# Sums of squares in an attention stage: transposes and a free-axis sum in place of products with a column of ones

## The chip, the core and the metric

The kernel runs on one core of a Trainium2 chip. The core has five engines, each with its own instruction queue that it works through in order: TensorE (PE in the profile; PEld is its loading of weights), VectorE (DVE), ScalarE (ACT), GpSimd (POOL) and SyncE (SP), which issues the DMAs. Engines wait for each other by semaphores. Products go into PSUM, eight banks of 128 x 512 float32. The metric is the time of one execution on the device in microseconds (us). The kernel before has a median of 1921.74 us over three runs (1920.86 to 1923.17).

## The reference

One layer: a normalised and modulated input of 1024 latent and 256 context tokens is projected, goes through two branches (A: a gated DeltaNet, B: differential attention), and both are merged. The change lies in branch B, behind the attention of each of the 8 heads:

```
def diff_attend(q, k, v, lam):              # per block of 128 queries
    s = jnp.einsum('bqhcd,bkhcd->bhcqk', qi, k) * scale     # c: two score maps
    p = jax.nn.softmax(s, axis=-1)
    attn = p[:, :, 0] - lam * p[:, :, 1]
    return jnp.einsum('bhqk,bkhv->bqhv', attn, v)           # 128 features a head
...
y_b = rms_norm(o_b, diff_norm_w) * (1.0 - lambda_init) * jax.nn.silu(z_b)
merged = g_a * (y_a @ w_oa) + g_b * (y_b @ w_ob)
```

`rms_norm(o_b)` needs, for each token and head, the sum of the squares of 128 features. How that sum is formed is what changes.

## The kernel before

The attention stage runs from about 1290 to 1750 us. A unit of work is a **tile**: 128 queries of one head, 64 tiles in all (8 heads of 8). Two tiles make a **pair**; there are 32 pairs, four to a head, counted here from the 1st to the 32nd. Head 0 has pairs 1 to 4, head 3 begins with pair 13, head 5 with pair 21, head 7 with pair 29.

A tile goes through these steps, and all of them are interleaved with other tiles:

- `scores` (L1615): 12 products `s` on TensorE, two for each of six pieces of 512, 512 and 256 keys for two score maps. VectorE moves each piece out of its bank with a scale and a minimum (`score_out`, L1642); three banks are shared.
- `soft` and `rel` (L1651, L1664): exponentials on ScalarE, small operations on VectorE.
- `scale` and `add` (L1673, L1681): one map scaled by -lambda times a ratio, on ScalarE or, for every fourth tile, on GpSimd, and the two added on GpSimd.
- `turns` (L1688): ten transposes `t` on TensorE, each of 128 x 128.
- `high` and `low` (L1706, L1718): ScalarE and VectorE split the transposed tile into two parts, `ah` and `al`.

A pair then goes through:

- `att_out` (L1726): 30 products `v` into the first 256 columns of a PSUM bank. This pool has one bank. Features lie on the partitions, the pair's 256 queries along the free axis.
- `out_pair` (L1743): ScalarE squares these 256 columns into `osq`.
- `gate_` (L1754): VectorE writes the gated output `oT`.
- `sum_` (L1763): the sum of squares over the partitions. TensorE multiplies each half of `osq` by a column of ones, `self.one`, into one column each of the same bank; VectorE scales the two columns, adds a small term `e2` and writes two columns of `ms`. With that and `oT` done, the bank is handed to the next pair (`self.vbank`).

After a head's fourth pair, `norm_` (L1786) raises `ms` to the power -0.5 on GpSimd (`bry`), transposes it on TensorE (`m<-ct,bry`), sends it through memory to every partition and multiplies `oT` by it.

Beside this runs `merge_` (L1870): 16 groups of 24 products `ma` of 512 columns, for branch A. They depend on little and fill TensorE between the steps of the attention. The last three groups are kept until all 64 tiles have been scored (`KEEP`, L1833, L1873). `merge_` and `norm_` take turns at one PSUM bank (`pbank`).

What sets the order is a planner in the kernel itself (`turn_flow`, L100). Each step is a generator that yields (engine, estimated time, dependencies, instruction); the planner keeps a clock for each engine and picks the step that can start earliest on it, with biases from `ABIAS`. So the numbers in a `yield` are no instructions, but a change of one of them, or one more step, may move all that follows. Two conditions hold steps back by plan alone: `over_` (L1760) lets the scores of head h begin only after the `norm_` of head h-2 has been planned to its end, and `norm_` needs the shared bank.

Of the kernel before, what the change touches and what calls it, by code (L numbers as in the profile page):

```python
# [12 lines left out]
ALU = mybir.AluOpType  # L13
AX = mybir.AxisListType
# [3 lines left out]
P = 128  # L18
# [11 lines left out]
W = 256  # L30
# [4 lines left out]
PE, DVE, ACT, POOL, DMA, ADMA, DV2, PL1 = range(8)  # L35
# [8 lines left out]
class Block:  # L44
# [1718 lines left out]
    def sum_(self, y, w, po, sq, t):  # L1763

        t0 = y["t"]
        e2 = self.a2.tile([P, 2], F32, tag="e2", name="e2")
        te = yield ACT, 0.13, [], lambda: self.nc.scalar.activation(e2, w["l0"][:, 0, t0:t0 + 2], AF.Square, scale=EPS ** 0.5)
        for j in range(2):
            t = yield PE, 0.11, [t], lambda: self.mm(po[:, W + j:W + j + 1], sq[:, j * P:(j + 1) * P], self.one)
        t = yield DVE, 0.075, [t, te], lambda: self.nc.vector.scalar_tensor_tensor(  # L1770
            w["ms"][:, t0:t0 + 2], po[:, W:W + 2], 1.0 / P, e2, ALU.mult, ALU.add)
        yield lambda: "o" in y
        self.vbank.append([t, y["o"]])
        if t0 == NL - 2:
            self.szfree = y["o"]
            self.norms.append((2 * y["i"] + 1, self.norm_(y["h"], w, t, y["o"])))
# [513 lines left out]
```

## Time and profile before

| | |
|---|---|
| median of three runs | 1921.74 us |
| the profiled execution, its span | 1923.5 us |
| TensorE busy | 1890.3 us (98%) |
| VectorE busy | 1458.9 us (76%) |
| ScalarE busy | 1079.6 us (56%) |
| GpSimd busy | 670.2 us (35%) |
| granted TensorE clock, mean | 0.998 |

The profile is of one execution. Its span, from the first to the last instruction, is 1.8 us above the median of the runs and within the three runs' spread by 0.4 us; there is no separate time around it in the profile. A row of the timeline has the start (us from the span's start), the duration, the engine, the line, the operation, the tiles as written<-read, the shape and how many instructions the row merges. A matmul's duration overlaps with the next one's, so what it occupies TensorE for is read from start to start. A row of the windows has, for each stretch, its length and the busy time of PE, PEld, DVE, ACT and POOL, then the granted clock, the DMA share and GB/s.

### The profile page before, as it was taken

To read this page: it belongs to the slowest core of one execution; us is meant where nothing else is said; L and a number is where in the kernel's file an instruction comes from. 1 tells how busy PE (TensorE), PEld (TensorE's weight loads), DVE (VectorE), ACT (ScalarE), POOL (GpSimd) and SP (SyncE) were. 2 spreads that over 40 slices of the span, in tenths; PEclk is the share of its full clock that TensorE was granted. 3 is DMA by queue.
4 is the path that set the end of the run, shared out by engine and by line. 5 is a ranking of instruction groups with operands and counts; after the bars stand their busy time and mean duration, and the time that the engine had idled before them with its cause. 6 is when DMAs were issued, how large, how long until landed. Compare 5 with 4: busy or idle time off the path is not lost.

```text
span 1923.5 us, 37549 instructions
## 1 busy us (share of the span) xinstructions
PE 1890.3 (98%) x13821; PEld 1663.8 (86%) x13821; DVE 1458.9 (76%) x3622; ACT 1079.6 (56%) x2241; POOL 670.2 (35%) x605
## 2 busy tenths in 40 slices
PE   7999999999999999999999999999999999999999
PEld 5988888899999998888888878888997988988887
DVE  5788998948886887767876756337996979995687
ACT  5553444426234563676776645548885868884222
POOL 2200000005541432343433232336666667672203
PEclk9999999999999999999999999999999999999999
DMA  9145534575546557667686555666436474226542
GB/s 337 62 134 113 140 92 123 132 205 170 175 132 204 156 194 229 231 196 251 198 274 203 196 179 157 205 227 232 136 122 212 159 241 159 84 89 217 181 161 88
DMA packets 383039, 336.39 MB, mean 175 GB/s; under 512 B 142609, under 2 KB 323443, under 8 KB 381831
## 3 DMA queue, kind: packets, MB, share of 16 engines
q1 hardware_dynamic: 382855, 333.99, 55.3%
q8 instruction: 109, 1.79, 0.4%
q14 instruction: 75, 0.61, 0.1%
HBM read 222.14 MB, written 111.79 MB: 174 GB/s over the span
## 4 chain that ended last, share of the span: by engine, by line
PE 56%; DVE 4%; ACT 2%; DMA 2%; issue 2%; POOL 1%; SPq 1%; ACTq 0%; DVEq 0%; POOLq 0%
PE mm L56 17%; PE s L56 7%; PE v L56 6%; PE chain L56 5%; PE mb L56 5%; PE ma L56 4%; PE x L56 3%; PE t L63 3%; PE out L56 3%; DVE S L1646 1%; PE gram L56 1%; PE z L56 1%; DVE al L1720 1%; DMA x<-xq 0%; ACT X L1310 0%
## 5 line engine op out<-in xcount | busy, mean ns | idle before, releaser
L56 PE MATMUL mm<-hs,wh 128*128 128x512 f32 (+1 forms) x2048 | 646.1, 389 | 1.2 <-ACT hs L453 1.2
L56 PEld LDWEIGHTS mm<-hs,wh 128*128 128x128 f32 x2048 | 371.9, 189 | 58.7 <-issue 2.0
L56 PE MATMUL mm<-hs,wl 128*128 128x512 f32 (+1 forms) x1024 | 397.8, 389 | 0.0
L56 PE MATMUL mm<-wh,hs 128*128 128x256 f32 (+1 forms) x1792 | 327.8, 283 | 0.8 <-ACT xc L649 0.6
L56 PEld LDWEIGHTS mm<-wh,hs 128*128 128x128 f32 x1792 | 276.8, 188 | 1.5 <-ACT xc L649 0.8
L56 PE MATMUL mm<-wl,hs 128*128 128x256 f32 (+1 forms) x896 | 253.6, 283 | 0.0
L1646 DVE TENSOR_SCALAR_CACHE_REDUCE S<-s,rsq 128x512 f32<-128x512 f32 (+1 forms) x384 | 239.0, 655 | 15.2 <-PE s L56 12.2
L1683 POOL TENSOR_TENSOR S<-S 128x1280 f32<-128x1280 f32 x64 | 188.9, 2957 | 92.0 <-ACT S L1676 90.8
L56 PEld LDWEIGHTS mm<-hs,wl 128*128 128x128 f32 x1024 | 193.9, 189 | 28.9 <-issue 0.9
L1659 ACT ACTIVATE S<-S,mn 128x1280 f32<-128x1280 f32 x128 | 175.2, 1371 | 51.1 <-DVE mn L1658 50.1
L56 PEld LDWEIGHTS mm<-wl,hs 128*128 128x128 f32 x896 | 168.8, 188 | 0.1
L661 DVE SCALAR_TENSOR_TENSOR ac<-xc,convT,ac 128x1284 f32<-128x1284 f32 (+1 forms) x96 | 138.8, 1448 | 14.1 <-ACT ac L659 13.5
L56 PE MATMUL s<-kk,qh 128*128 128x512 f32 (+1 forms) x384 | 142.1, 370 | 2.2 <-DVE S L1646 1.8
L56 PE MATMUL s<-kk,ql 128*128 128x512 f32 (+1 forms) x384 | 132.2, 356 | 0.0
L1720 DVE TENSOR_TENSOR al<-t,ah 128x512 fp32r<-128x512 f32 (+1 forms) x192 | 106.9, 595 | 7.0 <-ACT ah L1715 5.8
L646 POOL MEMSET xc<- 128x2 f32 (+1 forms) x64 | 3.5, 101 | 297.2 <-DMA gkk<-xc 117.7
L1231 DVE TENSOR_TENSOR tmp<-ab,ts 80x31 f32<-80x31 f32 (+15 forms) x248 | 94.1, 379 | 9.4 <-DMA ab<-da 3.8
L1364 POOL TENSOR_TENSOR x<-x,ct 128x256 f32<-128x256 f32 x64 | 47.7, 752 | 149.9 <-DMA x<-xq 107.9
L56 PE MATMUL ma<-y,wh 128*128 128x512 f32 x256 | 94.6, 414 | 1.8 <-DVE g L1893 1.8
L1233 DVE TENSOR_TENSOR ts<-ts,tmp 80x31 f32<-80x31 f32 (+15 forms) x248 | 91.3, 368 | 6.3
L1400 ACT ACTIVATE vd<-chain,edk 128x128 f32<-128x128 f32 x144 | 52.6, 371 | 76.5 <-PE chain L56 70.0
L1715 ACT CAST ah<-t 128x512 fp32r<-128x512 f32 (+1 forms) x192 | 88.1, 522 | 8.0 <-PE t L63 7.3
(307 smaller groups left out, 4356.2 us busy)
## 6 DMA issues: line engine op xcount, KB each, us to landing
wr<-in_w_in_dram SPq DMA_DIRECT2D x48, 512.0 KB, 5.8
hx<-in_w_in_dram SPq DMA_DIRECT2D x64, 256.0 KB, 4.7
x<-xq SPq DMA_DIRECT2D x64, 256.0 KB, 3.9
X<-gcd SPq DMA_DIRECT2D x8, 1280.0 KB, 10.6
kd<-col SPq DMA_DIRECT2D x40, 256.0 KB, 2.5
xq<-X SPq DMA_DIRECT2D x16, 640.0 KB, 4.5
kk<-kd SPq DMA_DIRECT2D x16, 640.0 KB, 5.7
kq<-gkq SPq DMA_DIRECT2D x8, 1152.0 KB, 8.4
```

Of the source, the lines that this page charges most:

```text
L56: self.nc.tensor.matmul(out, lhsT, rhs, start=start, stop=stop)
L63: self.nc.tensor.transpose(out, src, self.ident[:src.shape[0], :src.shape[0]])
L661: t = yield DV2, 1.21e-3 * wd, [t], lambda: nc.vector.scalar_tensor_tensor(ac[:, :wd], xc[:, j:j + wd], self.convw(j, x["ct"]), ac[:, :wd] ...
L1231: t = yield DV2, n * w / 960.0 + 0.08, [t if j else self.later(t, 2.5), t1], lambda: V.tensor_tensor(tv, ab[:, j + 1:, j:j + 1].to_broadca ...
L1233: t = yield DV2, n * w / 960.0 + 0.08, [t, t1], lambda: V.tensor_tensor(ts[:, j + 1:, :w], ts[:, j + 1:, :w], tv, ALU.subtract)
L1364: u["tqk"] = yield POOL, 0.72, [u["tx"]], lambda: nc.gpsimd.tensor_tensor(x[:, 1], x[:, 1], (self.up, self.lo)[d].unsqueeze(1).to_broadcas ...
L1400: td = yield ACT, 0.251, [t], lambda: nc.scalar.activation(vd, pc[:, 1], AF.Copy, scale=self.edk[:, c, g:g + 1])
L1646: e = yield DVE, 0.675 if m == 512 else 0.408, [e, self.sfree[c].get(n - 4 + c)], lambda: self.nc.vector.tensor_scalar(x["S"][c][:, o:o + ...
L1659: x["x"].append((yield ACT, 1.36, [e], lambda: nc.scalar.activation(S, S, AF.Exp, bias=x["mn"][:, c:c + 1], scale=-1.0, accum_out=w["l0"][ ...
L1683: e = yield POOL, 2.9, [e], lambda: self.nc.gpsimd.tensor_tensor(S0, S0, S1, ALU.add)
L1715: e = yield ACT, 0.48 if nb == 4 else 0.27, [t, y["old", k]], lambda: self.nc.scalar.copy(y["ah", k][:, :, q], pv)
L1720: t = yield DVE, 0.603 if k < 2 else 0.322, [e, y["old", k]], lambda: self.nc.vector.tensor_tensor(y["al", k][:, :, q], pv, y["ah", k][:, ...
```

## The change

In `sum_` the two products with a column of ones become two transposes of 128 x 128 (through `tr`, L62). They write 256 columns of the same bank, with the queries on the partitions; a new VectorE reduction sums them along the free axis into `ms`, and the scaling with the small term becomes an operation on `ms` alone. The bank is handed on after the reduction (`tb`) and `oT`.

```
         for j in range(2):
-            t = yield PE, 0.11, [t], lambda: self.mm(po[:, W + j:W + j + 1], sq[:, j * P:(j + 1) * P], self.one)
-        t = yield DVE, 0.075, [t, te], lambda: self.nc.vector.scalar_tensor_tensor(
-            w["ms"][:, t0:t0 + 2], po[:, W:W + 2], 1.0 / P, e2, ALU.mult, ALU.add)
+            t = yield PE, 0.109, [t], lambda: self.tr(po[:, W + j * P:W + j * P + P], sq[:, j * P:(j + 1) * P])
+        ms = w["ms"][:, t0:t0 + 2]
+        tb = t = yield DVE, 0.35, [t], lambda: self.nc.vector.tensor_reduce(
+            ms, po[:, W:2 * W].rearrange("p (j c) -> p j c", j=2), AX.X, ALU.add)
+        t = yield DVE, 0.075, [t, te], lambda: self.nc.vector.scalar_tensor_tensor(ms, ms, 1.0 / P, e2, ALU.mult, ALU.add)
         yield lambda: "o" in y
-        self.vbank.append([t, y["o"]])
+        self.vbank.append([tb, y["o"]])
```

The planner makes another order of the whole stage from this. Three places show it; in the rows, `s`, `t`, `v`, `ma` are the products and transposes named above, and x10 is ten in a row.

VectorE behind the 4th pair, before:

```order
L1646 TENSOR_SCALAR S,m_16021<-s,rsq 128x256
L1757 SCALAR_TENSOR_TENSOR oT<-v,dg,sz 128x256
L1720 TENSOR_TENSOR al<-t,ah 128x4x128 x2
L1770 SCALAR_TENSOR_TENSOR ms<-v,e_16107 128x2
L1720 TENSOR_TENSOR al<-t,ah 128x2x128
```

The same place in the changed kernel:

```order
L1646 TENSOR_SCALAR S,m_16026<-s,rsq 128x256
L1757 SCALAR_TENSOR_TENSOR oT<-v,dg,sz 128x256
L1720 TENSOR_TENSOR al<-t,ah 128x4x128 x2
L1771 TENSOR_REDUCE ms<-v 128x2
L1720 TENSOR_TENSOR al<-t,ah 128x2x128
L1773 SCALAR_TENSOR_TENSOR ms<-ms,e_16111 128x2
```

The reduction stands where the scaling stood, and the scaling comes one operation later.

TensorE between the 18th and the 19th pair's products, near the end of head 4, before:

```order
L56 MATMUL v<-ct,osq 128x1 x2
L56 MATMUL ma<-y,wl 128x512
L56 MATMUL ma<-y,wh 128x512 x2
L56 MATMUL ma<-y,wl 128x512
L56 MATMUL ma<-y,wh 128x512
L63 MATMUL t<-ct,S 128x128 x4
L56 MATMUL ma<-y,wh 128x512
L63 MATMUL t<-ct,S 128x128 x6
L56 MATMUL ma<-y,wl 128x512
L56 MATMUL ma<-y,wh 128x512 x2
L56 MATMUL ma<-y,wl 128x512
L56 MATMUL ma<-y,wh 128x512 x2
```

The same place in the changed kernel, up to the 19th pair's first product:

```order
L63 MATMUL v<-ct,osq 128x128 x2
L63 MATMUL t<-ct,S 128x128 x4
L63 MATMUL m<-ct,bry 8x128
L63 MATMUL t<-ct,S 128x128 x6
L56 MATMUL v<-ah,vh 128x256
```

Twelve products `ma` stood among the transposes; now none does, and the transpose of `norm_` has moved in.

TensorE behind the 27th pair, in head 6, before:

```order
L56 MATMUL v<-ct,osq 128x1 x2
L56 MATMUL ma<-y,wl 128x512
L63 MATMUL t<-ct,S 128x128 x4
L56 MATMUL ma<-y,wh 128x512
L63 MATMUL t<-ct,S 128x128 x6
L56 MATMUL ma<-y,wh 128x512
L56 MATMUL s<-kk,qh 128x512
L56 MATMUL s<-kk,ql 128x512
L56 MATMUL ma<-y,wl 128x512
L56 MATMUL ma<-y,wh 128x512
```

The same place in the changed kernel:

```order
L56 MATMUL v<-al,vh 128x256
L56 MATMUL v<-ah,vl 128x256
L63 MATMUL t<-ct,S 128x128 x10
L63 MATMUL v<-ct,osq 128x128 x2
L63 MATMUL t<-ct,S 128x128 x10
L56 MATMUL v<-ah,vh 128x256
```

Before, scores of head 7 and products `ma` stand between the pairs of head 6. Now the scores of head 7 begin only behind 25 of the 28th pair's 30 products, and from the 27th pair until the 30th pair's sums no `ma` is in the queue: 13 of the 16 groups have been used by the 26th pair's sums, and three are kept back.

Counted over both orders, heads 3 and 5 wait for the end of the head before them in both kernels; head 7 does so only in the changed one.

## The prediction

> **What bounds the kernel now.** I read the busy times first, then the attention stage by windows, then TensorE's and VectorE's timelines there. The order of TensorE in both kernels says which work can stand between which.
>
> ```profile
> PE 1890.3 (98%) x13821; PEld 1663.8 (86%) x13821; DVE 1458.9 (76%) x3622; ACT 1079.6 (56%) x2241; POOL 670.2 (35%) x605
> ```
> ```profile
> 1330.00:1440.00 110.00, 109.86 (x742) 99.01 (x741) 103.17 (x352) 93.45 (x157) 77.04 (x35) 1.00 0.44 146
> 1468.00:1498.00 30.00, 29.60 (x169) 24.70 (x168) 27.46 (x99) 22.79 (x35) 23.21 (x14) 1.00 0.44 150
> 1583.00:1614.00 31.00, 30.69 (x177) 26.06 (x175) 28.70 (x106) 24.26 (x39) 23.02 (x14) 1.00 0.46 151
> 1676.00:1703.00 27.00, 27.00 (x186) 24.58 (x184) 24.89 (x83) 22.80 (x41) 15.96 (x6) 1.00 0.18 56
> 1703.00:1747.00 44.00, 43.21 (x291) 37.80 (x291) 33.01 (x103) 33.23 (x59) 27.54 (x16) 1.00 0.32 110
> ```
>
> TensorE sets the pace (first busy time in each window), at a granted clock of 1.00. VectorE (third) is close behind: 103.17 of 110. So TensorE time removed is worth its full amount, as long as other work stands ready behind it; VectorE time added is free only inside gaps it has anyway.
>
> **TensorE's part of a pair.** Before, the sums of the 9th and of the 32nd pair (the rows with `osq`, four passes over the column of ones) with what follows them; then two transposes of a tile between products `ma`:
>
> ```profile
> 1430.81 0.50 PE L56 MATMUL v<-ct,osq 128*128 128x1 f32 x4
> 1431.17 0.72 PE L56 MATMUL ma<-y,wh 128*128 128x512 f32 x2
> 1431.73 0.40 PE L56 MATMUL ma<-y,wl 128*128 128x512 f32 x1
> 1431.96 0.40 PE L56 MATMUL s<-kk,qh 128*128 128x512 f32 x1
> ...
> 1436.32 0.28 PE L56 MATMUL v<-ah,vh 128*128 128x256 f32 x1
> ...
> 1746.21 0.50 PE L56 MATMUL v<-ct,osq 128*128 128x1 f32 x4
> 1746.58 0.70 PE L56 MATMUL ma<-y,wh 128*128 128x512 f32 x2
> 1747.12 0.40 PE L56 MATMUL ma<-y,wl 128*128 128x512 f32 x1
> ```
> ```profile
> 1420.36 0.38 PE L63 MATMUL t<-ct,S 128*128 128x128 f32 x2
> 1420.49 0.48 PE L56 MATMUL ma<-y,wl 128*128 128x512 f32 x1
> 1420.81 0.40 PE L56 MATMUL ma<-y,wh 128*128 128x512 f32 x1
> ```
>
> A 512-column product takes 0.23 (1431.73 to 1431.96). From the first sum to the third row it is 0.92 (1430.81 to 1431.73), and two products in it are 0.46, so the sums cost 0.46; at the 32nd pair 0.91 - 0.46 = 0.45. Two transposes with the product behind them take 0.45 (1420.36 to 1420.81), so the transposes alone cost 0.22. The new ones have the same shape and type. Saved: 0.23 x 32 pairs = **7.4 us**, all on the engine that bounds.
>
> The transposes' group row reads differently:
>
> ```profile
> L63 PE MATMUL t<-ct,S 128*128 128x128 f32 x640 | 86.6, 273 | 0.2
> ```
>
> 273 ns is each one's overlapped duration. [...] By that price two would cost 0.55, and the change would lose 0.1 x 32 = 3 us where I have it gain 7.4. The trace agrees with the 273 as a duration and not as an occupation (0.22 for two), and the clock stays at 1.00 in windows that hold dozens of transposes.
>
> **VectorE's part.** The trace has no sum of 2 x 128 out of PSUM. Two neighbours bound it:
>
> ```profile
> L1060 DVE TENSOR_REDUCE ss<-sq 128x8 f32<-128x512 f32 x20 | 13.7, 684 | 15.6 <-DMA vd<-vt 8.6 <-ACT sq L1050 6.6
> L1757 DVE SCALAR_TENSOR_TENSOR oT<-v,dg,sz 128x256 f32<-128x256 f32 x32 | 15.5, 484 | 36.5 <-ACT osq L1750 36.4
> ```
> ```profile
> 1341.79 0.48 DVE L1757 SCALAR_TENSOR_TENSOR oT<-v,dg,sz 128x256 f32<-128x256 f32 x1 [1.05 <-ACT osq L1750]
> 1342.19 0.15 DVE L1667 RECIPROCAL rl<-l 128x1 f32<-128x1 f32 x1
> ```
>
> Half the 512-element reduction is 0.34; a 256-column operation on the same bank occupies 0.40 (1341.79 to 1342.19). I take 0.35, as the first is the same operation; 0.34 to 0.40 are the ends. That is 11 us over 32 pairs. The scaling stays. What hides it is VectorE's wait before each `oT`, 36.5 us over 32 pairs or 1.1 a pair: there it waits for TensorE's last product `v`, so a delay of 0.35 earlier in the pair ends in that wait. Without this cover it would be up to 11 us; behind the reduction are the moves of `al`, for which the next pair's products wait. The bank of `v` is free 0.3 later, but at the 9th pair the next pair's first product (1436.32, above) comes 5.1 us after the sums (over at 1431.17), so nothing waits for it.
>
> **What the new order costs.** TensorE's queue is in order, so what counts is what stands between a head's last score and the next head's first pair. These rows are, for heads 2 to 3 and then 4 to 5: the last score, the last tile's first transposes, the next head's first score, its first pair's sums.
>
> ```profile
> 1440.50 0.28 PE L56 MATMUL s<-kk,ql 128*128 128x256 f32 x1
> ...
> 1454.63 0.60 PE L63 MATMUL t<-ct,S 128*128 128x128 f32 x4
> ...
> 1468.33 0.39 PE L56 MATMUL s<-kk,qh 128*128 128x512 f32 x1
> ...
> 1497.24 0.61 PE L56 MATMUL v<-ct,osq 128*128 128x1 f32 x4
> ...
> 1561.64 0.28 PE L56 MATMUL s<-kk,ql 128*128 128x256 f32 x1
> ...
> 1575.47 0.60 PE L63 MATMUL t<-ct,S 128*128 128x128 f32 x4
> ...
> 1583.49 0.39 PE L56 MATMUL s<-kk,qh 128*128 128x512 f32 x1
> ...
> 1613.80 0.50 PE L56 MATMUL v<-ct,osq 128*128 128x1 f32 x4
> ```
> ```profile
> 1440.00:1468.00 28.00, 13.02 (x46) 8.33 (x47) 1.38 (x2) 1.00 0.75 254
> 1468.00:1498.00 30.00, 10.65 (x36) 5.78 (x34) 1.38 (x2) 1.00 0.44 150
> 1562.00:1583.00 21.00, 9.39 (x31) 5.43 (x32) 0.69 (x1) 1.00 0.79 285
> 1583.00:1614.00 31.00, 10.22 (x35) 5.79 (x33) 0.69 (x1) 1.00 0.46 151
> ```
>
> The second view is the same windows for the tile `ma` alone. A drained tile needs 14.1 and 13.8 us from score to transposes (1440.50 to 1454.63, 1561.64 to 1575.47); a new head needs 28.9 and 30.3 us from its first score to its first sums. In both, 31 to 46 products `ma` a window fill TensorE, which is why its busy time there is nearly whole.
>
> Prices of the other steps come from these rows:
>
> ```profile
> 1440.62 0.28 PE L56 MATMUL v<-ah,vh 128*128 128x256 f32 x1
> 1440.73 0.28 PE L56 MATMUL v<-al,vh 128*128 128x256 f32 x1
> ...
> 1676.17 0.48 PE L56 MATMUL s<-kk,qh 128*128 128x512 f32 x1
> ...
> 1677.41 0.50 PE L56 MATMUL v<-ct,osq 128*128 128x1 f32 x4
> ```
>
> A `v` costs 0.117, a tile's twelve `s` 2.33 (twice 1676.17 to 1677.41, less the 0.08 that a product behind transposes takes longer), a transpose 0.11. Now I count the changed order.
>
> - *End of head 2* (last score to last tile): 33 `v`, 30 `t`, 16 `ma`, two sums and a small transpose are 11.4 us against 14.1 of latency, so 2.7 idle. Before: 39 `v`, 30 `t`, 14 `ma` and the rest, 12.1, so 2.0 idle. **+0.7.**
> - *End of head 4*: 33 `v`, 30 `t`, 10 `ma` and the rest, 10.0 against 13.8, so 3.8 idle; before 36 `v`, 30 `t`, 21 `ma`, 13.3, so 0.5. **+3.3.**
> - *End of head 6 and start of head 7*: new. From the last score of head 6 to the sums of the 29th pair, TensorE has 97 `v` (11.3), 67 `t` (7.4), six tiles of `s` (14.0), 2 `ma` (0.5) and the small rest (0.8): 34 us. The time it needs: 14 for the last tile, 5 for its ten transposes, the wait for `al` and 25 `v` ahead of head 7's first score, and 29 from that score to the sums; together 48. VectorE is busy for 27.46 of 30 and 28.70 of 31 us in such a start, so the missing `ma` do not shorten it much. That leaves 14 idle; the kernel before idles about 1 over this stretch (27.00 of 27 and 43.21 of 44 busy). I take **+12**, less than 13, because the latency was measured with `ma` in between. Bounds: 4 and 15.
>
> **The sum.** -7.4 + 0.7 + 3.3 + 12 = +8.6 us. The kept `ma` (three groups in both) still run at the end, so the tail behind the 32nd pair changes by less than 1. On the profile's own span, 1923.5, it gives 1932; on the median, 1921.74, **1930 us**, 0.4% slower.
>
> **Rivals.**
>
> - *The gaps shrink without `ma`* (the other side). If the drained tile's latency is set by products standing in front of it, not by ScalarE and GpSimd, it is shorter without them. The shortest from a tile's last score to the end of its add is 8.7 us:
>
> ```profile
> 1531.46 0.28 PE L56 MATMUL s<-kk,ql 128*128 128x256 f32 x1
> ```
> ```profile
> 1537.20 2.96 POOL L1683 TENSOR_TENSOR S<-S 128x1280 f32<-128x1280 f32 x1 [3.17 <-ACT S L1676]
> ```
>
>   With 10 for 14, the ends of heads 2 and 4 cost nothing more, and with a start of 24 to 28 in place of 29 the last gap costs 3 to 8: -7.4 + 3 to 8 is -4.4 to +0.6, 1917 to 1922. It is faster by more than 0.2% from the point where the new gap stays under 3.5 us. Against it: VectorE's share in the two starts, which no TensorE order removes.
> - *VectorE becomes the bound* in the filled pairs as well: 103.17 of 110 plus nine times 0.35 is 106.3, still under 110, so I doubt it. If none is hidden: +11, 1941.
> - *Transposes occupy TensorE for their whole 273 ns*: 0.55 a pair for 0.46, +3 in place of -7.4, 1941.
>
> That the change does not happen can be left out: the order shows the transposes and the reductions, 32 times each.
>
> **Chances.** The forecast, slower by 4 to 13: 0.57. The first rival: 0.33, of which 0.20 within 0.2% (3.8 us, about what a measurement can tell from no change) and 0.13 faster. VectorE: 0.06; transposes: 0.04. So slower 0.67, same 0.20, faster 0.13. The range reaches from the low half of the first rival to the forecast's own upper end with 15 in the new gap and 3 more for VectorE: 1918 to 1937.
>
> **What would show it.** Right: `v<-ct,osq` with half as many rows, one pair's sums at 0.22; a stretch around 1680 to 1715 with no `ma` and TensorE idle by some 12 us, ending at DVE or POOL rows; the reduction near 0.4 with the wait before `oT` down by about 10 us in total. Wrong: TensorE busy through the start of head 7, or idle spread evenly over all pairs with the wait before `oT` unchanged.

## The result, and the profile after

The changed kernel takes **1957.04 us** (median of four runs, 1955.74 to 1958.58), the kernel before 1921.42 in the same comparison: a ratio of 1.0177, 95% interval 1.0165 to 1.0188. The medians differ by 35.6 us, and the ratio makes it 34 (32 to 36). The direction was foreseen, the size was not: 1930 us was predicted, and the range ended at 1937.

An execution's span lies about 1.8 us below its time here (1956.8 us for 1958.58), so the profiled execution of the kernel before, with a span of 1923.5, took some 1925 us and lies a little above its three runs, not within them.

The page of the profiled execution (span 1956.8 us, granted clock 0.993 where before had 0.998), first its busy times. Behind it are the groups of the pair's last steps, with the busy time in us, the mean in ns, and the idle time ahead of them:

```profile
PE 1902.6 (97%) x13757; PEld 1660.3 (85%) x13757; DVE 1479.4 (76%) x3654; ACT 1080.5 (55%) x2241; POOL 671.1 (34%) x605
```
```profile
L1773 DVE SCALAR_TENSOR_TENSOR ms<-ms,e 128x2 f32<-128x2 f32 x32 | 19.4, 605 | 0.2
L1757 DVE SCALAR_TENSOR_TENSOR oT<-v,dg,sz 128x256 f32<-128x256 f32 x32 | 15.5, 484 | 37.2 <-ACT osq L1750 37.1
L1771 DVE TENSOR_REDUCE ms<-v 128x2 f32<-128x256 f32 x32 | 13.3, 416 | 1.4 <-PE v L63 1.4
```

and the same small operation in the kernel before:

```profile
L1770 DVE SCALAR_TENSOR_TENSOR ms<-v,e 128x2 f32<-128x2 f32 x32 | 5.0, 156 | 2.1 <-PE v L56 1.8
```

The reduction is what was expected. The scaling of two columns is not: it takes 605 ns on average where it took 156, 14.4 us more over 32 pairs. It is the same instruction on the same shape; what changed is that its first operand is `ms` in SBUF and no longer `v` in PSUM. VectorE, GpSimd and TensorE around its longest case:

```profile
1410.19 0.68 DVE L1895 TENSOR_TENSOR g<-ma,g 128x512 f32<-128x512 f32 x1
1410.79 2.77 DVE L1773 SCALAR_TENSOR_TENSOR ms<-ms,e 128x2 f32<-128x2 f32 x1
1413.48 1.01 DVE L1720 TENSOR_TENSOR al<-t,ah 128x512 fp32r<-128x512 f32 x2
```
```profile
1410.63 2.90 POOL L1683 TENSOR_TENSOR S<-S 128x1280 f32<-128x1280 f32 x1 [1.14 <-ACT S L1676]
```
```profile
1411.51 0.40 PE L56 MATMUL ma<-y,wl 128*128 128x512 f32 x1
1414.30 0.84 PE L63 MATMUL t<-ct,S 128*128 128x128 f32 x6 [2.40 <-DVE al L1720]
1414.90 1.01 PE L56 MATMUL ma<-y,wh 128*128 128x512 f32 x2
1415.71 0.63 PE L56 MATMUL s<-kk,qh 128*128 128x512 f32 x1
1416.14 0.63 PE L56 MATMUL s<-kk,ql 128*128 128x512 f32 x1
```

GpSimd begins its sum of `S` at 1410.63 and ends at 1413.53; the small operation begins at 1410.79 and ends at 1413.56. The other cases look the same. In the changed kernel 23 of the 32 small operations begin while a GpSimd instruction runs, and all 23 end 14 to 22 ns behind the end of one; the other nine meet none and take 149 to 163 ns. In the kernel before, with one operand in PSUM, 22 begin while one runs, and none of the 32 takes more than 161 ns.

In the case shown `al` stands behind the small operation in VectorE's queue, TensorE's transposes wait for `al`, and TensorE loses 2.40 us. The total of TensorE's waits for `al` ahead of transposes (us, times, the longest) says how often this happens; before has no row of this kind.

```profile
PE t L63 <- DVE al L1720: 11.4, 16, 2.4
```

The rows of TensorE above show a second loss: the two scores at 1415.71 and 1416.14 stand 0.43 apart, where 0.23 is usual. TensorE runs at half its rate until 1418.5; the granted clock, the third number from the end of this window's row, is 0.50:

```profile
1415.10:1418.50 3.40, 3.40 (x14) 2.92 (x13) 3.40 (x13) 2.50 (x4) 1.28 (x1) 0.50 0.28 77
```

Three theories were left for the whole of 34 us: the small operation's wait for GpSimd (P), the order of the work, which the prediction priced at 16 (O), and the transposes with their reduction. They can be taken apart because the order is the planner's and can be kept while the instructions are exchanged.

### The profile page after: what moved, and what is told of

It reads as the page before. It is cut to its first block, busy times and chain, and to the rows that moved or that the text cites. A ratio compares the mean times of both kernels' runs of the same rounds, so it can differ in the third digit from the quotient of the medians.

```text
span 1956.8 us, 37452 instructions
## 1 busy us (share of the span) xinstructions
PE 1902.6 (97%) x13757; PEld 1660.3 (85%) x13757; DVE 1479.4 (76%) x3654; ACT 1080.5 (55%) x2241; POOL 671.1 (34%) x605
## 4 chain that ended last, share of the span: by engine, by line
PE 47%; DVE 12%; ACT 3%; DMA 2%; issue 2%; POOL 1%; SPq 1%; ACTq 0%; DVEq 0%; POOLq 0%
PE mm L56 17%; PE chain L56 5%; DVE S L1646 5%; PE mb L56 4%; PE x L56 3%; PE ma L56 3%; PE v L56 3%; PE s L56 3%; DVE al L1720 3%; PE out L56 3%; PE t L63 2%; PE gram L56 1%; DVE ms L1773 1%; ACT S L1659 1%; PE z L56 1%
## 5 line engine op out<-in xcount | busy, mean ns | idle before, releaser
L661 DVE SCALAR_TENSOR_TENSOR ac<-xc,convT,ac 128x1284 f32<-128x1284 f32 (+1 forms) x96 | 138.8, 1448 | 12.2 <-ACT ac L659 11.6
L63 PE MATMUL t<-ct,S 128*128 128x128 f32 x640 | 90.2, 274 | 12.3 <-DVE al L1720 11.4
L1715 ACT CAST ah<-t 128x512 fp32r<-128x512 f32 (+1 forms) x192 | 89.4, 522 | 13.6 <-PE t L63 12.9
L56 PEld LDWEIGHTS s<-kk,qh 128*128 128x128 f32 x384 | 72.3, 188 | 28.9 <-DVE S L1646 18.6
```

The costliest lines, as they stand in the source:

```text
L56: self.nc.tensor.matmul(out, lhsT, rhs, start=start, stop=stop)
L63: self.nc.tensor.transpose(out, src, self.ident[:src.shape[0], :src.shape[0]])
L661: t = yield DV2, 1.21e-3 * wd, [t], lambda: nc.vector.scalar_tensor_tensor(ac[:, :wd], xc[:, j:j + wd], self.convw(j, x["ct"]), ac[:, :wd] ...
L1715: e = yield ACT, 0.48 if nb == 4 else 0.27, [t, y["old", k]], lambda: self.nc.scalar.copy(y["ah", k][:, :, q], pv)
```

## The experiments

In each diff, `-` is the kernel named, `+` the experiment. All ratios are to the kernel before, timed beside it.

### The small operation with one operand, in the changed order

```
-        t = yield DVE, 0.075, [t, te], lambda: self.nc.vector.scalar_tensor_tensor(ms, ms, 1.0 / P, e2, ALU.mult, ALU.add)
+        t = yield DVE, 0.075, [t, te], lambda: self.nc.vector.tensor_reduce(ms, ms.unsqueeze(2), AX.X, ALU.add)
```

> The changed kernel, in the same order, with its second VectorE operation on ms (two operands from SBUF) replaced by a sum over an axis of one, which reads ms alone; the scale 1/128 and the small term e2 are left out. Theory P (the port): the second operation waits for GpSimd's running instruction, 14.5 us in all, and the waits spread to TensorE. Expected by P: each second operation takes about 0.15 us, the time falls by 14 to 27 us, to 1930 to 1943. Theory O (the order): the loss comes from the new order alone. Expected by O: 1950 or more.

Measured: 1941.51 us, ratio 1.0093 (1.0078 to 1.0109), so 16 us of the loss went with one operand. This kernel leaves out the factor 1/128 and the small term. The group, and TensorE's waits for `al` and for the small operation:

```profile
L1773 DVE TENSOR_REDUCE ms<-ms 128x2 f32<-128x2 f32 x32 | 4.6, 145 | 0.1
```
```profile
PE t L63 <- DVE al L1720: 1.8, 4, 0.5
PE t L63 <- DVE ms L1773: 2.4, 5, 0.7
```

Every instruction stands at the same place, and the wait for `al` falls from 11.4 to 1.8. The row for the small operation itself had 0.3 us in the changed kernel, so of 11.7 us for both, 4.2 stay. P holds.

### The kernel before, with two operands in SBUF

```
-            w["ms"][:, t0:t0 + 2], po[:, W:W + 2], 1.0 / P, e2, ALU.mult, ALU.add)
+            w["ms"][:, t0:t0 + 2], e2, 1.0 / P, e2, ALU.mult, ALU.add)
```

> The kernel before, in the same order, with its one VectorE operation on ms reading e2 twice (two operands from SBUF) in place of the sums in PSUM and e2; so the sums are left out of ms. Expected by P: this operation lasts up to 3 us where GpSimd is busy, and the kernel is 8 to 25 us slower than before, 1930 to 1946. Expected by O: within 3 us of before.

Measured: 1941.90 us, ratio 1.0096 (1.0081 to 1.0111).

```profile
L1770 DVE SCALAR_TENSOR_TENSOR ms<-e 128x2 f32<-128x2 f32 x32 | 29.0, 908 | 0.0
```
```profile
PE t L63 <- DVE al L1720: 9.6, 12, 1.9
```

Here the order, the instruction and its shape stay as they were, and the place of one operand moved. With it the operation no longer reads the sums, so `ms` is without them, and the 2.1 us that it waited for TensorE's sums are gone too, which is no reason for a loss. The operation takes 908 ns on average and the kernel is 18 us slower, with 9.6 us of TensorE's waits for `al` that were not there. This shows P better than the experiment before it, which exchanged the instruction as well. Of the 32 operations 21 end 16 to 26 ns behind a GpSimd instruction that was running when they began; the other eleven take 148 to 157 ns, and of these nine met none and two began less than 25 ns before its end.

### The changed order with the instructions of before

```
-            t = yield PE, 0.109, [t], lambda: self.tr(po[:, W + j * P:W + j * P + P], sq[:, j * P:(j + 1) * P])
+            t = yield PE, 0.109, [t], lambda: self.mm(po[:, W + j:W + j + 1], sq[:, j * P:(j + 1) * P], self.one)
...
-        tb = t = yield DVE, 0.35, [t], lambda: self.nc.vector.tensor_reduce(
-            ms, po[:, W:2 * W].rearrange("p (j c) -> p j c", j=2), AX.X, ALU.add)
-        t = yield DVE, 0.075, [t, te], lambda: self.nc.vector.scalar_tensor_tensor(ms, ms, 1.0 / P, e2, ALU.mult, ALU.add)
+        tb = t = yield DVE, 0.35, [t], lambda: self.nc.vector.scalar_tensor_tensor(
+            ms, po[:, W:W + 2], 1.0 / P, e2, ALU.mult, ALU.add)
+        t = yield DVE, 0.075, [t, te], lambda: None
```

> The order of the changed kernel with the instructions of the kernel before: products with ones, one VectorE operation from PSUM where the reduction stood, nothing where the second operation stood. Expected by P: the order alone costs what the prediction's gaps say, up to 16 us, 1921 to 1938. Expected by O: 1945 or more, since the order holds the whole loss.

Measured: 1945.81 us, ratio 1.0116 (1.0098 to 1.0134). The time lies where O put it, and yet neither theory had it alone: the order by itself costs 22 us, and not the whole loss. The transposes with a reduction in place of the products win 4.3 us of it back (the first experiment, 1941.51, is this kernel with them; the runs of the two lie apart, 1940.68 to 1942.63 and 1943.11 to 1948.37, though the intervals of their ratios touch).

Where the order costs it shows in TensorE's unused time between the sums of two pairs: the time between them less the work there, at the prediction's prices (0.233 us for 512 columns, 0.117 for 256, 0.11 for a transpose). Half rate counts as unused in it. All are worked out from the traces, in us:

| stretch | before | order alone | with transposes, one operand | the changed kernel |
|---|---|---|---|---|
| pairs 1 to 9 | 1.4 | 1.4 | 2.9 | 9.9 |
| 9 to 13 (end of head 2) | 3.9 | 4.3 | 4.7 | 5.5 |
| 13 to 17 | 0.1 | 0.3 | 0.7 | 2.3 |
| 17 to 21 (end of head 4) | 1.4 | 5.1 | 5.4 | 7.3 |
| 21 to 25 | 0.5 | 0.2 | 0.7 | 2.9 |
| 25 to 29 (end of head 6, start of 7) | 1.2 | 11.8 | 12.9 | 13.4 |
| 29 to 31 | 1.9 | 1.7 | 2.2 | 2.2 |
| 31, and 25 us on | 0.7 | 8.2 | 7.7 | 9.4 |

Summed over the rows, 11.1 us are unused before, 33.0 with the order alone, 37.2 with the transposes and one operand, and 52.9 in the changed kernel. The steps are 21.9, 4.2 and 15.7; less the 7.4 us of TensorE's work that the transposes save, they make 34. The three gaps of the prediction are there, at 0.4, 3.7 and 10.6 us for 0.7, 3.3 and 12. The last row was not in it. These are the 25 us from the 31st pair's sums, as windows, before and with the order alone:

```profile
1737.00:1762.00 25.00, 23.97 (x130) 20.31 (x129) 16.57 (x24) 13.38 (x21) 4.18 (x3) 1.00 0.86 278
```
```profile
1752.00:1777.00 25.00, 19.55 (x97) 15.88 (x97) 14.96 (x21) 11.28 (x18) 3.41 (x2) 0.86 0.68 232
```

TensorE is busy 4.4 us less, at a granted clock of 0.86. In the changed kernel the same place reads, first on ScalarE, then on VectorE and on TensorE:

```profile
1774.08 1.04 ACT L1961 CAST yh<-yl 128x1024 fp32r<-128x1024 f32 x1 [4.85 <-DMA yl<-yb]
1775.37 1.05 ACT L1961 CAST yh<-yl 128x1024 fp32r<-128x1024 f32 x1 [0.24 <-DMA yl<-yb]
1776.72 1.04 ACT L1961 CAST yh<-yl 128x1024 fp32r<-128x1024 f32 x1 [0.31 <-DMA yl<-yb]
1777.68 0.38 ACT L1750 ACTIVATE osq<-v 128x256 f32<-128x256 f32 x1
```
```profile
1778.09 0.48 DVE L1757 SCALAR_TENSOR_TENSOR oT<-v,dg,sz 128x256 f32<-128x256 f32 x1 [0.36 <-ACT osq L1750]
```
```profile
1772.23 0.28 PE L56 MATMUL v<-ah,vl 128*128 128x256 f32 x1
...
1778.63 0.69 PE L63 MATMUL v<-ct,osq 128*128 128x128 f32 x2 [4.73 <-DVE oT L1757]
1778.97 0.78 PE L56 MATMUL ma<-y,wh 128*128 128x512 f32 x1
1779.54 0.63 PE L56 MATMUL ma<-y,wl 128*128 128x512 f32 x1
```

The last pair's product is issued at 1772.23, but its squares come at 1777.68: casts of the next stage (`yh<-yl`) stand ahead of them in ScalarE's queue and wait for a load. The gated output `oT` follows the squares, and the sums at 1778.63 follow `oT`, which the row names as their releaser. Before, one such cast stood there, and the squares came 0.3 us behind the last product.

### The tail, in three attempts

All three are built on the order alone. The first holds the casts back until the last pair's squares have been planned. On top of that the second plans the casts of the next weights 7 us later, so that ScalarE's queue has the six casts of outputs ahead of them; the third, in place of this, puts the stream that loads those weights (`wr`) ahead of the one that loads the stored outputs (`yl`).

```
+        self.squared = y["i"] + 1
...
+            yield lambda: self.squared == H * NL // 2
```
```
-                t1 = yield ACT, 0.52, [ts[m], self.wfree.get(14 + m)], lambda: nc.scalar.copy(hi[:, k], xr[:, m % 2, k])
+                t1 = yield ACT, 0.52, [self.later(ts[m], 7.0), self.wfree.get(14 + m)], lambda: nc.scalar.copy(hi[:, k], xr[:, m % 2, k])
```
```
-        for g, b in ((self.closing(zr, st, side), 200), (self.y_split(), 201), (self.b_weights(), 202), (self.forever(self.bouts), 203),
+        for g, b in ((self.closing(zr, st, side), 200), (self.y_split(), 202), (self.b_weights(), 201), (self.forever(self.bouts), 203),
```

> As k3_order_only (the changed order, the instructions of before), but the casts of y_split may be planned only behind the squares of the 32nd pair. Theory T: in the changed order three casts that wait for a DMA stand ahead of the last squares on ScalarE, and the 5 us that TensorE waits for these squares are part of the loss. Expected by T: 5 to 8 us below k3_order_only, 1937 to 1941. If the squares wait for something else: within 2 us of it.

> The changed order with the instructions of before, the casts of the stored outputs planned behind the last pair's squares as in the run before this one, and now the casts of the next weights (wh<-wr) planned 7 us later as well, so that on ScalarE all six casts of outputs stand ahead of the weights' casts; TensorE's and VectorE's rows stay as they were. Theory Q, the order of ScalarE's queue makes the tail: the wait of 6.06 us before mb<-yh,wl falls to 2 us or less and the median to between 1939 and 1943 (1946.5 without it). Rival L, the loads set the tail (six loads of yl and then those of wr on SyncE's queue, all behind the last pair's products): the wait stays above 4 us, and the median within 2 us of 1946.5.

> The changed order with the instructions of before and the casts of stored outputs behind the last pair's squares (1946.5 so far), and now the stream that loads the next stage's weights ahead of the one that loads the stored outputs: on SyncE's queue the two loads wr<-in_w_ob_dram stand ahead of the six yl<-yb, which wait for the last pair's products; TensorE's queue stays as it was. Theory L, the loads behind the last pair's products set the tail: the weights are issued some 10 us earlier, their casts no longer wait 6 us for them, the wait before the first mb (6.06 us) falls to under 2, and the median to between 1938 and 1943. Rival C, the chain of casts and subtractions behind the last squares is as long as the wait without any load in it (six casts of 1.05 and six subtractions of 1.22 us): the wait stays above 4 us, perhaps before another product mb, and the median within 2 us of 1946.5.

| kernel | median us, ratio to before |
|---|---|
| order alone | 1945.81, 1.0116 (1.0098 to 1.0134) |
| casts behind the squares | 1946.51, 1.0122 (1.0107 to 1.0137) |
| and the weights' casts later | 1944.78, 1.0113 (1.0096 to 1.0130) |
| casts behind the squares, weights loaded first | 1938.72, 1.0082 (1.0065 to 1.0098) |

The first two gained nothing that can be told. TensorE's rows show why, of the first and then of the second:

```profile
1775.14 0.79 PE L56 MATMUL mb<-yh,wl 128*128 128x512 f32 x1 [6.06 <-DVE wl L1984]
```
```profile
1772.73 0.50 PE L56 MATMUL mb<-yh,wh 128*128 128x512 f32 x1 [1.80 <-ACT wh L1983]
...
1777.00 0.80 PE L56 MATMUL mb<-yh,wl 128*128 128x512 f32 x1 [3.53 <-DVE wl L1984]
```

The sums no longer wait, but the wait comes back at the first products `mb` of the next stage, 6.06 us in the first attempt, 1.80 and 3.53 in the second. Neither order on ScalarE wins the time back. SyncE's queue of the kernel before, of the order alone and of the third attempt shows what lies behind it:

```profile
1740.12 5.08 SPq L1950 DMA_DIRECT2D yl<-yb  x6
1745.25 3.08 SPq L1970 DMA_DIRECT2D wr<-in_w_ob_dram  x2
```
```profile
1747.98 12.48 SPq L1952 DMA_DIRECT2D yl<-yb  x6
1760.51 2.97 SPq L1972 DMA_DIRECT2D wr<-in_w_ob_dram  x2
```
```profile
1747.60 1.21 SPq L1974 DMA_DIRECT2D wr<-in_w_ob_dram  x2
1748.85 11.11 SPq L1953 DMA_DIRECT2D yl<-yb  x6
```

With the order alone SyncE issues the first load of `yl` at 1747.98 and the second only at 1758.07, and the trace has the last of the six wait for the last pair's last product (1759.94); the loads of the next weights stood behind them. I read this as loads into memory that the attention still uses, which no run tests by itself. Issued at 1747.60 in place of 1760.51, they are there when they are needed; TensorE's row at the first `mb` shows no wait, and the 25 us from the 31st pair's sums, here as a window, are full at a clock of 1.00:

```profile
1769.35 0.39 PE L56 MATMUL mb<-yh,wh 128*128 128x512 f32 x1
```
```profile
1751.00:1776.00 25.00, 23.47 (x128) 19.84 (x127) 14.75 (x22) 11.41 (x19) 4.08 (x3) 1.00 0.66 222
```

The time unused there falls from 8.2 to 1.4 us and the kernel's by 7.1 (6.5 by the ratios). So the tail's 7.5 us are a hand-over to the next stage: loads queued behind others that wait for the last pair, and casts queued ahead of its squares. The third attempt also moved one cast of the weights on ScalarE and two of their subtractions on VectorE forward, and the loads were not moved without the first attempt, so what each part is worth by itself stays open. Before, the same order of loads cost nothing: 36 products `ma` stood behind the last sums there, where the changed order has 26, and fewer casts stood ahead of the squares. Which of these two decided it wasn't tried.

### A planner that knows of the wait

The planner has a class for VectorE operations, `DV2`, that it keeps clear of GpSimd's (L119). Other operations with two operands in SBUF, such as L661, are planned in it; the new one was planned as plain `DVE`.

```
-        t = yield DVE, 0.075, [t, te], lambda: self.nc.vector.scalar_tensor_tensor(ms, ms, 1.0 / P, e2, ALU.mult, ALU.add)
+        t = yield DV2, 0.075, [t, te], lambda: self.nc.vector.scalar_tensor_tensor(ms, ms, 1.0 / P, e2, ALU.mult, ALU.add)
```

> The changed kernel with the second operation planned as one that keeps clear of GpSimd (the planner has such a class, DV2); a new order follows. Expected by P: most of the waits in the second operation go, 1925 to 1945. Expected by O: no reason for a gain, 1950 to 1965.

Measured: 1933.57 us, ratio 1.0049 (1.0034 to 1.0064); another class for one operation takes 23 us off the changed kernel (some 24 by the ratios).

```profile
L1773 DVE SCALAR_TENSOR_TENSOR ms<-ms,e 128x2 f32<-128x2 f32 x32 | 7.6, 238 | 0.0
```

The wait is nearly gone (238 ns), and the order is another one: the 32nd pair's sums come at 1753.85, for 1778.63 in the changed kernel. Since both changed, this run doesn't separate them.

### Once a head, without the plan's wait, and spread

The next kernels mend rather than separate. The first takes the operation out of `sum_` and does it once a head in `norm_`, on eight columns; the second also drops the condition that holds the scores of head h until the `norm_` of head h-2; the third raises `PACE`, so that the planner uses the products `ma` earlier.

```
+        e = yield DV2, 0.08, [t, te], lambda: nc.vector.scalar_tensor_tensor(w["ms"], w["ms"], 1.0 / P, e2, ALU.mult, ALU.add)
...
-            yield lambda: "in" in self.aT.get(h, ()) and self.turned > n - 4 and self.added > n - 3 and (t or self.over_(h))
+            yield lambda: "in" in self.aT.get(h, ()) and self.turned > n - 4 and self.added > n - 3
...
-    PACE = 4.48
+    PACE = 7.5
```

> The changed kernel with the scaling and the small term applied once a head to eight columns, in place of once a pair to two; everything is computed. The order is a new one: in it heads 2 and 4 wait for the end of the head before, and no ma stands behind the 24th to 30th pair. Theory P: 8 in place of 32 operations with two operands from SBUF, so at most 8 waits, planned clear of GpSimd: no spread loss. With the price of the remaining gaps 1922 to 1940. If transposes and reductions as such cost the 35 us: 1950 or more.

> As f1_once_a_head, and the scores of a head may be planned before the normalisation of the head two before it is. Theory G (the gaps): in this order no head waits for the end of the one before, ma stands in every pair, and 120 ma are left for the end; TensorE idles little, so 1906 to 1921, below the kernel before. If VectorE bounds the pairs with the reduction in them: 1925 or more.

> The changed kernel with the second VectorE operation once a head and without the plan's wait of a head for the end of the head before it (1925.5 so far, TensorE idle 5.4 us in the 25 us behind the last sums, at four changes of the one bank of ma), and PACE 7.5 in place of 4.48, so that the planner uses the products ma earlier: 66 in place of 133 are left behind the last sums. If the time of that kernel beyond TensorE's own work lies in those waits for the bank, the median falls to between 1917 and 1923, below both kernels. If VectorE's time in the filled pairs sets it, the stall moves ahead of the last sums and the median stays between 1924 and 1930.

The kernel before was given the same two edits of the plan, one after the other:

> The kernel before with the same condition taken away from its scores. Theory G: its idle time of about 11 us in the stage is an upper bound of the gain, 1911 to 1921. Against f3_no_head_wait this shows transposes and reductions alone without gaps and without the wait for GpSimd: by the prediction's sum f3 is 7 us lower if the reductions are hidden, 4 us higher if none is.

> The kernel before with the same two edits of the plan (no wait of a head for the one before it, PACE 7.5; 1929.7 with the first alone): products with a column of ones, one VectorE operation a pair. If the spread helps the order and not the transposes, it falls by as much as the changed kernel with the same edits, and stays 3 to 6 us above it; if VectorE sets the time, it comes out at or below that kernel, having 0.33 us a pair less work on VectorE.

| edits | with transposes, once a head | with the column of ones |
|---|---|---|
| none of the plan | 1934.24, ratio 1.0056 (1.0041 to 1.0071) | the kernel before |
| no wait of a head | 1925.54, 1.0011 (1.0001 to 1.0021) | 1929.69, 1.0032 (1.0021 to 1.0043) |
| and `PACE` 7.5 | 1919.29, 0.9987 (0.9978 to 0.9996) | 1926.55, 1.0027 (1.0017 to 1.0036) |

The gap theory as it was put for the second row (1906 to 1921 and 1911 to 1921) fell. The transposing kernel came out where VectorE as the bound had been put (1925 or more), and its spread version where the waits for the bank had been put (1917 to 1923), which speaks against VectorE. Without the plan's wait the attention ends far earlier, with the 32nd sums at 1717.22 in the transposing kernel for 1746.21 before, but the products `ma` left over then run alone behind one bank and stop for it. The idle time in the group of `ma<-y,wh` has these stops, first in that kernel and then in the spread version:

```profile
L56 PE MATMUL ma<-y,wh 128*128 128x512 f32 x256 | 93.6, 420 | 5.3 <-DVE g L1895 5.3
```
```profile
L56 PE MATMUL ma<-y,wh 128*128 128x512 f32 x256 | 93.1, 414 | 1.0 <-DVE g L1895 1.0
```

Spreading them takes 4.3 of the 5.3 us away and brings 1919.29 us. It is the only version that lies below the kernel before, by 0.13% (0.04 to 0.22), about what a measurement can just tell. The second and the third row were timed in different comparisons, so the steps between them are taken from the ratios: the spread wins 0.24% (4.6 us) here and 0.05% (1.0 us) with the column of ones, which was to fall by as much and did not. Within the third row the column of ones ends 7.3 us higher (1926.55), a little more than the 3 to 6 that were expected of it; within the second row it is 4.2 us, where 7 had been put if the reductions are hidden.

## Why the prediction was wrong

The steps in their order, and what the runs showed:

- **TensorE, -7.4 us: right.** In the changed kernel a pair's two transposes occupy 0.22, worked out as in the prediction (median); the products occupy 0.44 to 0.45. In whole times: the transposes with a reduction take 4.3 us less than the products in the same order (1941.51 for 1945.81), 4.2 less without the plan's wait (1925.54 for 1929.69) and 7.3 less where the order is spread too (1919.29 for 1926.55); each kernel has its own order in the last two. The rival of 273 ns each fell.
- **VectorE's reduction, 0.35, hidden: right in size, and nearly in effect; wrong in where.** It occupies 0.33 and costs about 3 us (7.4 less 4.3). But the wait before `oT`, which was to shrink by 10, didn't: 36.5 us before, 35.8 with the order alone and with the reduction. Nor is it a wait for TensorE's last product, as the prediction read it: its row names ScalarE's squares, and in all 32 pairs of the kernel before `oT` begins 0.03 us behind the end of its pair's squares. What shrank in the attention stage are VectorE's waits for `ah`, here with the order alone and then with the reduction:

```profile
DVE al L1720 <- ACT ah L1715: 12.2, 23, 1.5
```
```profile
DVE al L1720 <- ACT ah L1715: 7.3, 14, 1.5
```

- **"The scaling stays": this step failed.** It was counted at nothing beyond its 0.15 us because the operation was the same. Its operand had moved from PSUM to SBUF, and with two SBUF operands it waited out a running GpSimd instruction in 23 of 32 cases: 14.4 us on VectorE and 16 us in the time (1957.04 to 1941.51). GpSimd's share, 77.04 of 110 us, stood in the prediction's first windows. The operation took 605 and 908 ns on average with two SBUF operands (the changed kernel, the second experiment) and 156 with one of them in PSUM (before); the reduction of one SBUF operand took 145 (the first experiment).
- **The order, +0.7, +3.3 and +12: right.** 0.4, 3.7 and 10.6 were measured, 14.7 for 16. The first rival, that the gaps shrink without `ma`, fell: 11.8 us stayed unused from the 25th to the 29th pair.
- **"The tail behind the 32nd pair changes by less than 1": failed, by 7.5 us.** I counted groups of `ma` kept back (three in both) and followed neither the products left behind the last sums (36 and 26) nor ScalarE's and SyncE's queues into the next stage. The third attempt on the tail gives 7.1 us back and leaves TensorE's order as it was, but for one small transpose of the last `norm_`.

With the two failed steps put right, the sum is 8.6 + 16 + 7.5 = 32; with the reduction's 3 us and 1.3 less for the gaps it is 34, for the 34 to 36 measured. A part of these terms is the clock. The changed kernel's windows over pairs 1 to 9 and 25 to 29 read

```profile
1329.00:1439.00 110.00, 105.64 (x678) 91.57 (x677) 102.51 (x332) 86.59 (x147) 71.77 (x34) 0.98 0.42 146
1682.00:1739.00 57.00, 51.49 (x308) 40.99 (x308) 47.92 (x159) 42.17 (x71) 34.88 (x20) 0.97 0.29 93
```

with 0.98 and 0.97 where before had 1.00; the prediction's sum has no term for it. In this execution's stage the granted clock was 0.50 from 1415.1 to 1418.5, 1575.5 to 1578.9, 1698.4 to 1701.8 and 1776.9 to 1787.1, together 20.4 us. TensorE was busy for 17.6 of them, so an estimate of what the clock cost is half of that at most, 9 us. The order alone and the first experiment have 10.2 us of this kind each, the kernel before none. These microseconds lie inside the terms above and are not to be added to them.

## What to carry to other kernels

When an operation "stays", look at where each of its operands now lies: a two-column operation lasted 2.77 us here because it waited out a GpSimd instruction of 2.90, and all that was queued behind it paid. Follow every queue, SyncE's too, through the hand-over to the next stage, since a load behind one that waits comes late as well (issued at 1760.51 here, and at 1747.60 when it stood ahead). Where a planner sets the order, time the new order with the old instructions too: here it cost 22 us, while the edit itself saved 4 to 7.

## What the hardware showed unasked

- A VectorE scalar_tensor_tensor of 128 x 2 with both operands in SBUF ended 14 to 26 ns behind the end of a running GpSimd instruction, after up to 2.77 us, in 44 of 64 cases (two executions); in the other 20 it took 148 to 163 ns. With one operand in PSUM the mean of 32 is 156 ns.
- TensorE's granted clock was 0.50 for 3.4 us (1415.1 to 1418.5, 0.43 us a 512-column product for 0.23) behind 3.0 us without a product: 2.40 us of pause and six transposes (1411.9 to 1414.90, above). What lowers the clock is not shown: in the same execution 3.3 us (from 1451.1) and 3.9 us (from 1704.0) in which TensorE had transposes, pauses and no product left the granted clock at 1.00, while in the spread version products of 512 columns took 0.43 us for 0.23 from 1742.33 to 1744.9, behind a pause of 2.07 us that ended at 1741.02.
